# Half of the gate's contraction as seven block products of 160 tokens, and the feed-forward in three parts

## The chip, the cores and the metric

The kernel runs on one core of one Trainium2 chip. Its time is the device time of one execution in microseconds. Two executions of the kernel before took 1676.51 and 1676.54 us, so their median is 1676.53 us. A third execution was recorded by the hardware profiler; it took 1677.32 us, and the span from its first to its last instruction is 1675.2 us.

## The reference

One layer of a decoder (a short gated convolution and a sliding-window attention side by side, merged, then a feed-forward) on 256 prompt tokens and 64 sample tokens, 320 in all. What the change touches is the feed-forward at the end:

```python
h = x + merged @ w_o
hn = rms_norm(h, g_ffn)
h = h + (jax.nn.silu(hn @ w_gate) * (hn @ w_up)) @ w_down
```

The model width is 2048, the feed-forward's inner width 5632. Everything is in 32-bit floats.

## The kernel before, in words

**Products by three passes.** Activations are held feature by feature: a tile has 128 features on the partitions and the 320 tokens (`T`) along the free axis. Each 32-bit operand is split into a high part in the matmul's reduced 32-bit format and a low part that holds the remainder (`split_to`: ScalarE copies the high part, VectorE subtracts to get the low one). A product is then three matmuls: high by high, weight high by activation low, weight low by activation high. Each matmul has a stationary operand of 128x128 weights, which is loaded for that matmul alone, also where two matmuls in succession use the same weights.

**`product`** (L127 to L150) computes two output chunks of 128 features for all tokens. It takes the contraction of 2048 features (`KC` = 16 chunks) in four weight tiles of four chunks each. Per weight tile: SyncE starts a transfer of 512 KB into a `wraw` tile (four buffers), ScalarE writes `whi`, VectorE writes `wlo` (three buffers each), and TensorE runs 24 matmuls of 320 tokens. A `wraw` buffer is free for its next transfer when both halves of its split are done; a `whi` or `wlo` buffer is free when the last matmul that reads it is done. The function `passes` orders the matmuls, with the low-weight pass up to three places (`LAG`) behind the others and four of them at the end of a tile.

**The feed-forward** (L894 to L976) goes through the 44 chunks of the inner width in two parts of 28 and 16 chunks (`FH`). In each part it takes two chunks at a time: a gate product (`fg`, 96 matmuls), the SiLU on VectorE and ScalarE (`gs`, `sg`), an up product (`fu`, 96 matmuls), and the result, split, into the big tile `a_t`. After each part `down` (L844) multiplies `a_t` by the down weights, 512 output features per call, and adds the result to the residual stream `hT`. The last call of the second part is written out by itself (L979 to L1047): its weights are prepared ahead in tiles that have come free (`held`), and 128 of the tokens are accumulated by rows in a PSUM bank that stays reserved (`rowacc`).

**PSUM.** `product` and `down` draw on a pool of four banks (`acc`). A second pool, `aux2`, has three banks.

**The order of the work.** The kernel is written against a framework that records the instructions, sorts them per engine with a scheduler of its own before the program runs, and puts in the semaphore waits. On the chip each engine then works through its list in the order that was fixed; ScalarE and VectorE do not overtake a waiting instruction. The framework treats a PSUM bank as a whole: a matmul that writes to a bank waits for earlier reads of it by other engines, whichever columns they read.

**`wo`** (L810 to L829): the product before the feed-forward. Its eviction adds to `hT` and writes the feed-forward's input, scaled by `g_ffn` and split, to `hh_t` and `hl_t`.

Of the kernel before, what the change touches and what calls it, by code (L numbers as in the profile page):

```python
# [36 lines left out]
E0 = D - 512  # L37
TR = T - P
XB = [1, 1, 2, 2, 2, 2, 2, 4]
TOK = [(0, 128), (128, 128), (256, 64)]  # L40


@with_exitstack
def hybrid_layer(ctx: ExitStack, tc: tile.TileContext, a: dict, o: list):
# [18 lines left out]
    def ps_aux(name):  # L63
        return aux[0].tile([P, 512], F32, tag="aux", name=name)
# [120 lines left out]
    rbsq = cst.tile([P, T], F32, name="rbsq")  # L185
    rbq = cst.tile([P, T], F32, name="rbq")

    def rstd_of(ss, shape, name, pool, out=None):

# [38 lines left out]
    vT = zz.tile([P, 2, T], F32, name="vT")  # L228
    vn = [zz.tile([P, DKV], F32, name=f"vn{t}") for t in range(3)]
    xacc = zz.tile([P, T], F32, name="xacc")  # L230
    rel = zz.tile([NBK, NH], F32, name="rel")
    oh = zz.tile([NBK, WIN], F32, name="oh")
    rel_r = zz.tile([NBK, 2, NH], F32R, name="rel_r")
# [573 lines left out]
    rb2 = hp.tile([P, T], F32, name="rb2")  # L807
    hh_t = xp.tile([P, KC, T], F32R, tag="xh", name="hh_t")
    hl_t = xp.tile([P, KC, T], F32R, tag="xl", name="hl_t")
    for mp in range(8):  # L810
        c0 = mp * CW
        ps = product(
            lambda k0, n: load_cols(w_o, k0, n, c0), KC,
            lambda k: m_h[:, k, :], lambda k: m_l[:, k, :], "wo",
        )
        for c in range(2):
            k = mp * 2 + c
            nc.vector.tensor_add(hT[:, k, :], ps[c][:, :T], hT[:, k, :])
            nc.scalar.activation(hh_t[:, k, :], hT[:, k, :], AF.Copy, scale=g_ffn[:, k:k + 1])
            nc.vector.scalar_tensor_tensor(  # L820
                hl_t[:, k, :], hT[:, k, :], g_ffn[:, k:k + 1], hh_t[:, k, :].bitcast(F32),
                op0=ALU.mult, op1=ALU.subtract,
            )
            if k == 0:
                nc.gpsimd.tensor_tensor(hacc, hT[:, k, :], hT[:, k, :], op=ALU.mult)
            else:
                t = tmp("tc", "sq")[:, :T]
                nc.gpsimd.tensor_tensor(t, hT[:, k, :], hT[:, k, :], op=ALU.mult)
                nc.gpsimd.tensor_tensor(hacc, hacc, t, op=ALU.add)  # L829
    mp_.close()  # L830


# [9 lines left out]
    ylow = op.tile([P, E0], F32, name="ylow")  # L842

    def down(half, c0):  # L844

        nf, f0 = FH[half], half * FH[0]
        ps = [ps_acc(u("dn")) for _ in range(4)]
        low = ps_aux(u("dl")) if c0 < E0 else rowacc
        sets = [[k] for k in range(0, nf, 2)]
        sets[-2:] = [sets[-2] + sets[-1]]  # L850
        for i, k0s in enumerate(sets):
            parts = {}
            for k0 in k0s:
                raw = wp.tile([P, 2, 512], F32, tag="wraw", name=u("wraw"), bufs=4)
                nc.sync.dma_start(raw, w_d[c0 // 512, :, f0 + k0:f0 + k0 + 2, :])
                hi = wp.tile([P, 2, 512], F32R, tag="whi", name=u("whi"), bufs=3)
                lo = wp.tile([P, 2, 512], F32R, tag="wlo", name=u("wlo"), bufs=3)
                split_to(hi, lo, raw)
                for j in range(2):
                    parts[k0 + j] = (hi[:, j, :], lo[:, j, :])  # L860
            end = i == len(sets) - 1
            order = [(k, c) for k in parts for c in range(4)]
            if end or i == 0:
                order.sort(key=lambda kc: kc[1])
            for k, c, m in passes(order, end):
                cs = slice(c * P, (c + 1) * P)
                if m == 0:
                    nc.tensor.matmul(  # L868
                        ps[c], parts[k][0][:, cs], a_t[:, k, 0:512], start=k == 0, stop=False
                    )  # L870
                elif m == 1 and c == 0:
                    nc.tensor.matmul(  # L872
                        low, a_t[:, k, 512:], parts[k][0], start=k == 0, stop=k == nf - 1 and c0 < E0
                    )
                elif m == 2:
                    last["mm"] = nc.tensor.matmul(  # L876
                        ps[c][:, :T], parts[k][1][:, cs], a_t[:, k, 0:T], start=False, stop=k == nf - 1
                    )
            if pending and i % 2 == 1:
                with after(last["lo"], last["mm"]):  # L880
                    pending.pop(0)()
        mark["out"] = []
        for c in range(4):
            k = c0 // P + c
            nc.vector.tensor_add(hT[:, k, :], hT[:, k, :], ps[c][:, :T])
            mark["out"].append(nc.vector.tensor_add(hT[:, k, P:T], hT[:, k, P:T], ps[c][:, T:]))
        if c0 < E0:
            ys = ylow[:, c0:c0 + 512]
            if half == 0:
                nc.scalar.activation(ys, low, AF.Copy)  # L890
            else:
                nc.vector.tensor_add(ys, low, ys)

    for half in range(2):  # L894
        f0 = 0 if half == 0 else FH[0]
        nf = FH[half]

        a_big = fp.tile([P, FH[0], 2 * T], F32R, tag="at", name=u("a_t"))
        a_t = a_big[:, :nf, :]
        for fpair in range(nf // 2):  # L900
            c0 = (f0 + fpair * 2) * P
            psg = product(
                lambda k0, n: load_cols(w_g, k0, n, c0), KC,
                lambda k: hh_t[:, k, :], lambda k: hl_t[:, k, :], "fg",
            )
            if half == 0 and fpair == 0:
                pss = ps_aux("pss2")
                over_partitions(pss[:, :T], two_parts(hacc, ("tc", "td")))
                rstd_of(pss[:, :T], [P, T], "r2", hp, out=rb2)
            gs = []  # L910
            for c in range(2):
                t, t2 = tmp("ta", "gs")[:, :T], tmp("tb", "sg")[:, :T]
                nc.vector.tensor_mul(t, psg[c][:, :T], rb2)
                last["sig"] = nc.scalar.activation(t2, t, AF.Sigmoid)
                nc.vector.tensor_mul(t, t, t2)
                nc.vector.tensor_mul(t, t, rb2)
                gs.append(t)
            psu = product(
                lambda k0, n: load_cols(w_u, k0, n, c0), KC,
                lambda k: hh_t[:, k, :], lambda k: hl_t[:, k, :], "fu",  # L920
            )
            for c in range(2):
                nc.vector.tensor_mul(gs[c], psu[c][:, :T], gs[c])
                f = fpair * 2 + c
                last["hi"] = nc.scalar.activation(a_t[:, f, 0:T], gs[c], AF.Copy)
                for t0, t1, d0 in ((P, T, T), (0, P, 512)):
                    last["lo"] = nc.vector.tensor_sub(
                        a_t[:, f, d0:d0 + t1 - t0], gs[c][:, t0:t1], a_t[:, f, t0:t1].bitcast(F32)
                    )
        if half == 1:  # L930
# [4 lines left out]
            yacc = op.tile([P, TR], F32, name="yacc")  # L935

            def row_squares(i, src):
                jk = op.tile([P, 512], F32, tag="jk", name=u("jk"))
                nc.scalar.activation(jk, src, AF.Square, accum_out=ssf[:, i:i + 1])

            def rows_of(c0):
# [27 lines left out]
            with after(last["sig"]):  # L969
                nc.scalar.activation(warm, ones, AF.Sqrt)  # L970

        for c0 in range(0, D if half == 0 else E0, 512):
            down(half, c0)
            if half == 1:
# [4 lines left out]
    nf = FH[1]  # L979
    es = slice(E0, D)  # L980

    held = []
    free = a_big[:, nf:, :].rearrange("p k t -> p (k t)")
    more = xp.tile([P, 4 * KT * CW], F32R, tag="xl", name="more")
    for j in range(nf // 2):
        raw = wp.tile([P, 2, 512], F32, tag="wraw", name=u("wraw"), bufs=4)
        nc.sync.dma_start(raw, w_d[E0 // 512, :, FH[0] + 2 * j:FH[0] + 2 * j + 2, :])
        if j < 5:
            src, n = (free, 2 * j) if j < 3 else (more, 2 * (j - 3))
            hi, lo = (  # L990
                src[:, i * KT * CW:(i + 1) * KT * CW].rearrange("p (k n) -> p k n", k=2) for i in (n, n + 1)
            )
# [160 lines left out]
```

## Time and profile before

| | value |
|---|---|
| median of two executions | 1676.53 us |
| profiled execution | 1677.32 us |
| its span | 1675.2 us |
| mean granted TensorE clock | 0.999 |
| matmuls | 10967 |
| read from memory | 253.3 MB, 154 GB/s over the span |

How to read the rows that follow: times are microseconds from the start of the span unless marked ns. PE is TensorE's matmuls, PEld its loads of stationary operands, DVE VectorE, ACT ScalarE, SPq the queue of SyncE, which starts the transfers. `L141` is a line of the kernel. A group's row gives the line, the engine, the operation, the tile written and the tiles read, partitions x elements, and the count; then the busy time in us, the mean duration of one in ns, and the idle time of the engine just ahead of them. Matmuls are pipelined, so the duration of one (309 ns for 320 tokens) is longer than the distance to the next.

### The profile page before, as it was taken

What the parts mean: (1) busy time and instruction counts of PE and PEld (TensorE: products, weight loads), DVE (VectorE), ACT (ScalarE), POOL (GpSimd) and SP (SyncE); (2) the same over time, 40 slices, a digit from 0 to 9 for tenths busy, and PEclk for the clock granted to TensorE, in tenths of its full rate; (3) what the DMA queues carried; (4) which work ended last, traced back from release to release, by engine and by line L of the source; (5) the groups of instructions that cost most, each with busy time, mean ns of one, the idle gap of its engine ahead of it and who ended that gap; (6) DMA issues with size and microseconds to landing.
All of it is one profiled execution on the core that took longest, in us unless ns stands there. A gap on an engine that the chain in (4) does not pass through costs nothing.

```text
span 1675.2 us, 26334 instructions
## 1 busy us (share of the span) xinstructions
PE 1664.8 (99%) x10967; PEld 1620.0 (97%) x10967; DVE 893.5 (53%) x1293; ACT 650.9 (39%) x861; POOL 79.5 (5%) x120
## 2 busy tenths in 40 slices
PE   9999999999999999999999999999999999999998
PEld 9999999999999999999999999998888999999887
DVE  7779555444444445556555555553444455555556
ACT  6545343333333333334333333333333333334442
POOL 0101311000000002320000000000000000000000
PEclk9999999999999999999999999999999999999999
DMA  7544545544444444444444444444444444444552
GB/s 256 169 154 140 178 137 183 162 149 149 151 152 151 151 149 149 149 148 150 151 151 151 151 150 148 149 148 151 150 151 151 151 150 151 151 152 151 176 164 88
DMA packets 73390, 258.12 MB, mean 154 GB/s; under 512 B 8440, under 2 KB 10920, under 8 KB 73144
## 3 DMA queue, kind: packets, MB, share of 16 engines
q1 hardware_dynamic: 71160, 250.28, 45.1%
q0 software_dynamic: 1968, 5.90, 1.2%
q8 instruction: 86, 1.41, 0.3%
q14 instruction: 32, 0.26, 0.0%
q10 hardware_dynamic: 144, 0.26, 0.0%
HBM read 253.30 MB, written 5.08 MB: 154 GB/s over the span
## 4 chain that ended last, share of the span: by engine, by line
PE 99%; DMA 0%; ACT 0%; SPq 0%; DVE 0%; issue 0%; DVEq 0%
PE fg L141 18%; PE fu L141 18%; PE dn L868 9%; PE ga L141 7%; PE wo L141 7%; PE gc L141 7%; PE dn L876 6%; PE B L141 3%; PE C L141 3%; PE q L141 3%; PE yc L141 3%; PE H L141 3%; PE ya L141 3%; PE dl L872 2%; PE kv L311 1%; PE dn L1011 1%
## 5 line engine op out<-in xcount | busy, mean ns | idle before, releaser
L95 DVE TENSOR_TENSOR wlo<-wraw,whi 128x1024 fp32r<-128x1024 f32 (+1 forms) x459 | 561.8, 1224 | 636.6 <-ACT whi L94 630.0
L94 ACT ACTIVATE whi<-wraw 128x1024 fp32r<-128x1024 f32 (+1 forms) x459 | 485.5, 1059 | 780.0 <-PE dn L868 157.8
L868 PE MATMUL dn<-a_t,whi 128*128 128x512 f32 x640 | 218.8, 394 | 0.0
L141 PE MATMUL fg<-hh_t,whi 128*128 128x320 f32 x704 | 212.4, 309 | 0.0
L141 PE MATMUL fu<-hh_t,whi 128*128 128x320 f32 x704 | 212.4, 309 | 0.0
L141 PE MATMUL fg<-hl_t,whi 128*128 128x320 f32 x704 | 212.3, 309 | 0.0
L141 PE MATMUL fu<-hl_t,whi 128*128 128x320 f32 x704 | 212.3, 309 | 0.0
L141 PE MATMUL fg<-hh_t,wlo 128*128 128x320 f32 x704 | 164.0, 309 | 0.0
L141 PE MATMUL fu<-hh_t,wlo 128*128 128x320 f32 x704 | 164.0, 309 | 0.0
L876 PE MATMUL dn<-a_t,wlo 128*128 128x320 f32 x640 | 152.0, 309 | 0.0
L868 PEld LDWEIGHTS dn<-a_t,whi 128*128 128x128 f32 x640 | 119.3, 188 | 23.5
L141 PEld LDWEIGHTS fg<-hh_t,whi 128*128 128x128 f32 x704 | 132.2, 188 | 0.0
L141 PEld LDWEIGHTS fu<-hh_t,whi 128*128 128x128 f32 x704 | 132.2, 188 | 0.0
L141 PEld LDWEIGHTS fu<-hl_t,whi 128*128 128x128 f32 x704 | 132.2, 188 | 0.0
L141 PEld LDWEIGHTS fg<-hl_t,whi 128*128 128x128 f32 x704 | 132.2, 188 | 0.0
L876 PEld LDWEIGHTS dn<-a_t,wlo 128*128 128x128 f32 x640 | 112.4, 188 | 10.9
L141 PEld LDWEIGHTS fg<-hh_t,wlo 128*128 128x128 f32 x704 | 118.5, 188 | 0.0
L141 PEld LDWEIGHTS fu<-hh_t,wlo 128*128 128x128 f32 x704 | 118.5, 188 | 0.0
L141 PE MATMUL ga<-xh_t,whi 128*128 128x320 f32 x256 | 77.3, 310 | 0.0
L141 PE MATMUL gc<-xh_t,whi 128*128 128x320 f32 x256 | 77.3, 310 | 0.0
L141 PE MATMUL ga<-xl_t,whi 128*128 128x320 f32 x256 | 77.3, 310 | 0.0
L141 PE MATMUL gc<-xl_t,whi 128*128 128x320 f32 x256 | 77.3, 310 | 0.0
(310 smaller groups left out, 2748.1 us busy)
## 6 DMA issues: line engine op xcount, KB each, us to landing
wraw<-in_w_in_dram SPq DMA_DIRECT2D x128, 512.0 KB, 3.8
wraw<-in_w_gate_dram SPq DMA_DIRECT2D x88, 512.0 KB, 3.7
wraw<-in_w_up_dram SPq DMA_DIRECT2D x88, 512.0 KB, 3.7
wraw<-in_w_down_dram SPq DMA_DIRECT2D x88, 512.0 KB, 3.4
wraw<-in_w_o_dram SPq DMA_DIRECT2D x32, 512.0 KB, 3.7
wraw<-in_w_conv_out_dram SPq DMA_DIRECT2D x16, 512.0 KB, 3.6
wraw<-in_w_attn_out_dram SPq DMA_DIRECT2D x16, 512.0 KB, 3.5
wraw<-in_w_kv_dram SPq DMA_DIRECT2D x7, 512.0 KB, 7.8
```

The lines of the kernel that those rows point to most:

```text
L94: last["hi"] = nc.scalar.activation(hi, src, AF.Copy)
L95: last["lo"] = nc.vector.tensor_sub(lo, src, hi.bitcast(F32))
L141: last["mm"] = nc.tensor.matmul(ps[c][:, :T], w[:, k, c * P:(c + 1) * P], x(kc), start=(kc == 0 and i == 0), stop=(kc == nk - 1 and i == 2),)
L311: last["mm"] = nc.tensor.matmul(ps[c][:, :T], w[:, k, c * P:(c + 1) * P], x(kc), start=(kc == 0 and m == 0), stop=(kc == KC - 1 and m == 2),)
L868: nc.tensor.matmul(ps[c], parts[k][0][:, cs], a_t[:, k, 0:512], start=k == 0, stop=False)
L872: nc.tensor.matmul(low, a_t[:, k, 512:], parts[k][0], start=k == 0, stop=k == nf - 1 and c0 < E0)
L876: last["mm"] = nc.tensor.matmul(ps[c][:, :T], parts[k][1][:, cs], a_t[:, k, 0:T], start=False, stop=k == nf - 1)
L1011: nc.tensor.matmul(ps[c][:, :2 * TR], held[k][0][:, cs], a_t[:, k, P:512], start=k == 0, stop=False)
```

## The change

In 21 of the 22 gate products (all but the first of the first part), half of the contraction is computed by another scheme. Two contraction chunks and two output chunks form a 2 by 2 grid of weight blocks, and the tokens are halved into two blocks of 160 (`T2`). Strassen's scheme, in the form with shared sums, gives the four results of such a grid from seven block products in place of eight. Four of the eight pairs of contraction chunks (`NS`) go this way, in two weight tiles (`by_seven(0)`, `by_seven(1)`); the other two tiles of a gate product are computed as before (`plain`).

For it the kernel prepares, once, sums and differences of the scaled activations of the first eight chunks (`sums_of`, after the first four `wo` products), and, in each of the two weight tiles of each gate product, four sums of weight blocks (`tw`), which are then split like the weights (`thi`, `tlo`, one buffer each). The seven products of three passes each are 42 matmuls of 160 tokens per weight tile. They accumulate in column ranges of three banks (`pa`, `pb`, `pc`, all three of `aux2`); the plain tiles accumulate in columns 0 to 319 of `pa` and `pb`. One result of the seven is read out by ScalarE, and four short VectorE operations combine it with others, ahead of the last plain tile in the text; two VectorE additions follow after it.

The feed-forward is cut into three parts of 16, 14 and 14 chunks in place of 28 and 16. This frees memory for the sums. The activations for the first weights are scaled into a temporary and split from there; some temporaries move to other tiles.

The core of the diff:

```diff
+    sums = hp.tile([P, 2, NS, 4, T2], F32R, tag="sums", name="sums")
+
+    def sums_of(pair, xs):
+        d = hp.tile([P, 4, T2], F32, tag="tw", name=u("sx"), bufs=2)
+        x0, x1 = xs
+        nc.vector.tensor_sub(d[:, 0], x0[:, T2:], x1[:, T2:])
+        nc.vector.tensor_sub(d[:, 2], x0[:, T2:], x0[:, :T2])
+        nc.vector.tensor_sub(d[:, 1], x0[:, :T2], d[:, 0])
+        nc.vector.tensor_sub(d[:, 3], x1[:, :T2], d[:, 1])
+        split_to(sums[:, 0, pair], sums[:, 1, pair], d)
...
-            nc.scalar.activation(hh_t[:, k, :], hT[:, k, :], AF.Copy, scale=g_ffn[:, k:k + 1])
-            nc.vector.scalar_tensor_tensor(
-                hl_t[:, k, :], hT[:, k, :], g_ffn[:, k:k + 1], hh_t[:, k, :].bitcast(F32),
-                op0=ALU.mult, op1=ALU.subtract,
-            )
+            xs = tmp(("ta", "tb")[c], "xs")[:, :T]
+            nc.scalar.activation(xs, hT[:, k, :], AF.Copy, scale=g_ffn[:, k:k + 1])
+            split_to(hh_t[:, k, :], hl_t[:, k, :], xs)
+            scaled.append(xs)
...
+        if mp < NS:
+            sums_of(mp, scaled)
...
-    FH = (28, 16)
+    FH = (16, 14, 14)
...
+    def gate_product(c0):
+        pa, pb, pc = (ps_aux(u(n)) for n in ("ga_", "gb_", "gc_"))
+        sl = lambda p, i: p[:, i * T2:(i + 1) * T2]
+        P3, P5, P2, Q4, P1, P6, P7 = sl(pb, 0), sl(pb, 2), sl(pa, 0), sl(pa, 1), sl(pa, 2), sl(pc, 0), sl(pc, 1)
...
+        def by_seven(tile_i):
+            raw = raw_tile()
+            mark["load"] = nc.sync.dma_start(raw, w_g[c0 // CW, :, tile_i * KT:(tile_i + 1) * KT, :])
+            r4 = raw.rearrange("p (a k) (n m) -> p a (k n) m", k=2, n=2)
+            tw = hp.tile([P, 2, 4, P], F32, tag="tw", name=u("tw"), bufs=2)
+            rh, rl = (x.rearrange("p (a k) (n m) -> p a (k n) m", k=2, n=2) for x in part_tiles())
+            th, tl = (fp.tile([P, 2, 4, P], F32R, tag=t, name=u(t)) for t in ("thi", "tlo"))
+
+            nc.vector.tensor_add(
+                tw[:, :, 0:2], r4[:, :, 0:1].to_broadcast([P, 2, 2, P]), r4[:, :, 1:3]
+            )
+            nc.vector.tensor_add(tw[:, :, 2], tw[:, :, 0], r4[:, :, 2])
+            nc.vector.tensor_add(tw[:, :, 3], tw[:, :, 2], r4[:, :, 3])
+            split_to(rh[:, :, 1:4], rl[:, :, 1:4], r4[:, :, 1:4])
+            split_to(th, tl, tw)
...
+                for out, bank, w, x in (
+                    (P1, "pa", W(rh, rl, 1), h(k, 0)), (P2, "pa", W(rh, rl, 3), h(k + 1, 0)),
+                    (P3, "pb", W(rh, rl, 2), d(3)), (P5, "pb", W(th, tl, 0), d(0)),
+                    (P7, "pc", W(th, tl, 1), d(2)), (P6, "pc", W(th, tl, 2), d(1)),
+                    (Q4, "pa", W(th, tl, 3), h(k + 1, 1)),
+                ):
+                    seq += [(out, bank, w[0], x[0]), (out, bank, w[0], x[1])]
+                    low.append((out, bank, w[1], x[0]))
...
+        by_seven(0)
+        plain(2, False)
+        by_seven(1)
+
+        p1, nw, n = q[:, 0], q[:, 1], q[:, 2]
+        nc.scalar.activation(p1, P1, AF.Copy)
+        nc.vector.tensor_sub(n, p1, P6)
+        nc.vector.tensor_sub(nw, n, P7)
+        nc.vector.tensor_sub(t0[:, 0:T2], P5, n)
+        nc.vector.tensor_sub(t0[:, T2:T], P5, nw)
+        plain(3, True)
+        nc.vector.tensor_add(t1, pa[:, 0:T], q[:, 0:2].rearrange("p a t -> p (a t)"))
+        nc.vector.tensor_add(t0, pb[:, 0:T], t0)
+        return t0, t1
...
-    for half in range(2):
-        f0 = 0 if half == 0 else FH[0]
-        nf = FH[half]
+    for half, nf in enumerate(FH):
+        f0 = F0[half]
...
-            psg = product(
-                lambda k0, n: load_cols(w_g, k0, n, c0), KC,
-                lambda k: hh_t[:, k, :], lambda k: hl_t[:, k, :], "fg",
-            )
             if half == 0 and fpair == 0:
+                psg = product(
+                    lambda k0, n: load_cols(w_g, k0, n, c0), KC,
+                    lambda k: hh_t[:, k, :], lambda k: hl_t[:, k, :], "fg",
+                )
...
+            else:
+                psg = gts = gate_product(c0)
```

More of the change, by code (lines that the diff above doesn't have):

```diff
@@ L39 @@
 XB = [1, 1, 2, 2, 2, 2, 2, 4]
+T2 = T // 2
+NS = 4
 TOK = [(0, 128), (128, 128), (256, 64)]
@@ L230, in hybrid_layer @@
     xacc = zz.tile([P, T], F32, name="xacc")
+    rbsq = zz.tile([P, T], F32, name="rbsq")
+    rbq = zz.tile([P, T], F32, name="rbq")
     rel = zz.tile([NBK, NH], F32, name="rel")
@@ L815, in hybrid_layer @@
         )
+        scaled = []
         for c in range(2):
@@ L839, in hybrid_layer, with plain @@
     op = ctx.enter_context(tc.tile_pool(name="op", bufs=1))
-    FH = (28, 16)
+    FH = (16, 14, 14)
+    F0 = [sum(FH[:i]) for i in range(len(FH))]
+    END = len(FH) - 1
     ylow = op.tile([P, E0], F32, name="ylow")
+    def gate_product(c0):
+        pa, pb, pc = (ps_aux(u(n)) for n in ("ga_", "gb_", "gc_"))
+        sl = lambda p, i: p[:, i * T2:(i + 1) * T2]
+        P3, P5, P2, Q4, P1, P6, P7 = sl(pb, 0), sl(pb, 2), sl(pa, 0), sl(pa, 1), sl(pa, 2), sl(pc, 0), sl(pc, 1)
+        fresh = {"pa": pa, "pb": pb, "pc": pc}
+        t0, t1 = (tmp("ta", "gs")[:, :T] for _ in range(2))
+        q = fp.tile([P, 3, T2], F32, tag="q", name=u("q"))
+        mm = lambda out, w, x, bank, stop: nc.tensor.matmul(
+            out, w, x, start=fresh.pop(bank, None) is not None, stop=stop, skip_group_check=True
+        )
[13 more added lines that the diff above has]
+            split_to(th, tl, tw)
+            seq, low = [], []
+            for a in range(2):
+                pair = tile_i * 2 + a
+                k = 2 * pair
+                h = lambda k, i: tuple(x[:, k, i * T2:(i + 1) * T2] for x in (hh_t, hl_t))
+                d = lambda i: (sums[:, 0, pair, i], sums[:, 1, pair, i])
+                W = lambda x, y, i: (x[:, a, i], y[:, a, i])
+                for out, bank, w, x in (
[6 more added lines that the diff above has]
+                    low.append((out, bank, w[1], x[0]))
+                    if len(low) > LAG:
+                        seq.append(low.pop(0))
+            for out, bank, w, x in seq + low:
+                last["mm"] = mm(out, w, x, bank, False)
+        def plain(tile_i, end):
+            hi, lo = load_cols(w_g, tile_i * KT, KT, c0)
+            order = [(k, c) for k in range(KT) for c in range(2)]
+            if end:
+                order.sort(key=lambda kc: -kc[1])
+            for k, c, i in passes(order, end):
+                kc = tile_i * KT + k
+                w, x = ((hi, hh_t), (hi, hl_t), (lo, hh_t))[i]
+                last["mm"] = mm(
+                    (pb if c == 0 else pa)[:, 0:T], w[:, k, c * P:(c + 1) * P], x[:, kc, :], None,
+                    end and k == KT - 1 and i == 2,
+                )
+        by_seven(0)
[11 more added lines that the diff above has]
+        return t0, t1
@@ L844, in down @@
     def down(half, c0):
-        nf, f0 = FH[half], half * FH[0]
+        nf, f0 = FH[half], F0[half]
         ps = [ps_acc(u("dn")) for _ in range(4)]
@@ L872, in down @@
                     nc.tensor.matmul(
-                        low, a_t[:, k, 512:], parts[k][0], start=k == 0, stop=k == nf - 1 and c0 < E0
+                        low, a_t[:, k, 512:], parts[k][0], start=k == 0 and (c0 < E0 or half == 0),
+                        stop=k == nf - 1 and c0 < E0
                     )
@@ L901, in hybrid_layer @@
             c0 = (f0 + fpair * 2) * P
-            psg = product(
-                lambda k0, n: load_cols(w_g, k0, n, c0), KC,
-                lambda k: hh_t[:, k, :], lambda k: hl_t[:, k, :], "fg",
-            )
             if half == 0 and fpair == 0:
+                psg = product(
+                    lambda k0, n: load_cols(w_g, k0, n, c0), KC,
+                    lambda k: hh_t[:, k, :], lambda k: hl_t[:, k, :], "fg",
+                )
+                psg = [p[:, :T] for p in psg]
                 pss = ps_aux("pss2")
                 over_partitions(pss[:, :T], two_parts(hacc, ("tc", "td")))
-                rstd_of(pss[:, :T], [P, T], "r2", hp, out=rb2)
+                rstd_of(pss[:, :T], [P, T], "r2", spare, out=rb2)
+                gts = [tmp("ta", "gs")[:, :T] for _ in range(2)]
+            else:
+                psg = gts = gate_product(c0)
             gs = []
             for c in range(2):
-                t, t2 = tmp("ta", "gs")[:, :T], tmp("tb", "sg")[:, :T]
-                nc.vector.tensor_mul(t, psg[c][:, :T], rb2)
+                t, t2 = gts[c], tmp("tb", "sg")[:, :T]
+                nc.vector.tensor_mul(t, psg[c], rb2)
                 last["sig"] = nc.scalar.activation(t2, t, AF.Sigmoid)
@@ L929, in hybrid_layer @@
                     )
-        if half == 1:
+        if half == END:
             ya = xp.tile([P, 2, D], F32, tag="xh", name="ya")
@@ L937, in row_squares @@
             def row_squares(i, src):
-                jk = op.tile([P, 512], F32, tag="jk", name=u("jk"))
+                jk = hp.tile([P, 512], F32, tag="tw", name=u("jk"), bufs=2)
                 nc.scalar.activation(jk, src, AF.Square, accum_out=ssf[:, i:i + 1])
@@ L970, in hybrid_layer @@
                 nc.scalar.activation(warm, ones, AF.Sqrt)
-        for c0 in range(0, D if half == 0 else E0, 512):
+        for c0 in range(0, D if half < END else E0, 512):
             down(half, c0)
-            if half == 1:
+            if half == END:
                 pending.append(lambda c0=c0: rows_of(c0))
                 pending.append(lambda c0=c0: rest_of(range(c0 // P, c0 // P + 4)))
-    nf = FH[1]
+    nf = FH[END]
     es = slice(E0, D)
-    held = []
-    free = a_big[:, nf:, :].rearrange("p k t -> p (k t)")
-    more = xp.tile([P, 4 * KT * CW], F32R, tag="xl", name="more")
+    held, places = [], []
+    more = xp.tile([P, 5 * KT * CW], F32R, tag="xl", name="more")
+    free = hp.tile([P, 5 * KT * CW], F32R, tag="sums", name="free")
+    for x in (more, free, a_big[:, nf:, :].rearrange("p k t -> p (k t)")):
+        places += [
+            x[:, i:i + KT * CW].rearrange("p (k n) -> p k n", k=2)
+            for i in range(0, x.shape[-1] - KT * CW + 1, KT * CW)
+        ]
     for j in range(nf // 2):
         raw = wp.tile([P, 2, 512], F32, tag="wraw", name=u("wraw"), bufs=4)
[L987 to L992, printed above, removed]
+        nc.sync.dma_start(raw, w_d[E0 // 512, :, F0[END] + 2 * j:F0[END] + 2 * j + 2, :])
+        if len(places) > 1:
+            hi, lo = places.pop(0), places.pop(0)
         else:
```

2 lines of the change are left out of this document (removed).

## The prediction

> **What bounds the kernel now.** I read the summary and the chain of waits first, then the chain in one stretch of the feed-forward.
>
> ```profile
> span 1675.2 us, 26334 instructions
> ...
> PE 1664.8 (99%) x10967; PEld 1620.0 (97%) x10967; DVE 893.5 (53%) x1293; ACT 650.9 (39%) x861; POOL 79.5 (5%) x120
> ...
> PE 99%; DMA 0%; ACT 0%; SPq 0%; DVE 0%; issue 0%; DVEq 0%
> ```
>
> ```profile
> 947.94 14.08 PE fu L141 x96
> 962.02 14.08 PE fg L141 x96
> ```
>
> ```profile
> 962.02:976.10 14.08, 14.08 (x98) 14.08 (x98) 7.02 (x10) 5.20 (x7) 0.00 (x0) 1.00 0.43 153
> sum 28.16, PE 28.16 PEld 28.16 DVE 14.50 ACT 10.39 POOL 0.00; mean PE 14.08 PEld 14.08 DVE 7.25 ACT 5.20 POOL 0.00
> ```
>
> The first two rows of the summary say that TensorE works without a break, and the chain is TensorE alone. In the feed-forward a product of 96 matmuls takes 14.08 us, 146.7 ns for each matmul of 320 tokens, with no wait in it. One gate and one up product are 28.16 us (the sum row, its columns PE, PEld, DVE, ACT in order), in which VectorE works 14.5 us and ScalarE 10.4. So the time changes by what TensorE's list changes, and by any wait that the change puts into it.
>
> **TensorE's work.** A gate product keeps 48 of its 96 matmuls and does the other 48 as 84 matmuls of 160 tokens. Whether that saves depends on the distance between two short matmuls, each with its own load. The nearest rows:
>
> ```profile
> 1640.74 0.25 PE L1015 MATMUL dn<-a_t 128*128 128x192 f32 x1
> ...
> 1640.83 0.36 PE L1011 MATMUL dn<-a_t 128*128 128x384 f32 x1
> ...
> 1641.03 0.59 PE L1015 MATMUL dn<-a_t 128*128 128x192 f32 x4
> ...
> 1641.45 0.60 PE L945 MATMUL fa<-ident,xv 128*128 128x128 f32 x4
> ```
>
> ```profile
> 116.80 0.82 PE L518 MATMUL pp<-ident,s 128*128 128x128 f32 x6
> ```
>
> ```profile
> L518 PE MATMUL pp<-ident,s x48: 271/272/330, 116.8 to 174.1; 128*128 128x128 f32 x48
> ```
>
> A single matmul of 192 tokens between longer ones takes 90 ns (1640.74 to 1640.83). Four in a row take 0.42 us (1641.03 to 1641.45); with 90 for the first, 110 for each that follows. Six transposes of 128 columns take 0.82 us; less the last one's 0.27, five distances of 110. So in a run the distance does not fall with the width below about 110 ns: it is the load of the next weights that sets it, and PEld is as busy as PE in the sum row. A `by_seven` tile is a run of 42. I take 111 ns, with 105 (the mean of the four) and 113 as bounds. Per gate product: 84 x 111 ns = 9.32 us in place of 48 x 146.7 ns = 7.04, so 2.28 us more, and in 21 products **47.9 us more**. The bounds give 37 and 51.
>
> [...]
>
> **The wait that the change adds.** The built program's order around one gate product, VectorE's list and then ScalarE's (`8345` the last plain tile, `8389` and `8419` the first two tiles of the up product, `8521` to `8527` the first tile of the *next* gate product):
>
> ```
> wlo_8390<-wraw_8387,whi_8389      whi_8389<-wraw_8387
> tw_8523<-wraw_8521   (three)      whi_8419<-wraw_8417
> wlo_8420<-wraw_8417,whi_8419      thi_8526<-tw_8523
> tlo_8527<-tw_8523,thi_8526        q_8195<-ga__1044_8190   (P1)
> q, q, gs, gs         (the four)   whi_8449<-wraw_8447
> ```
>
> TensorE's list has, behind the second `by_seven` tile, three matmuls of the up product, 12 of the last plain tile into `pa` (they wait for ScalarE's read of P1, from the same bank), three more of the up product, 12 into `pb` (they wait for the four on VectorE). So P1's read is queued behind `thi_8526`, that behind `tw_8523`, and that behind the transfer of `wraw_8521`. The up product's tiles hold all four `wraw` buffers, and the first is free when `wlo_8390` is done: VectorE frees a buffer and then waits for what is loaded into it.
>
> ```profile
> 941.49 1.23 DVE L95 TENSOR_TENSOR wlo<-wraw,whi 128x1024 fp32r<-128x1024 f32 x1 [2.29 <-ACT whi L94]
> 942.75 3.80 SPq L99 DMA_DIRECT2D wraw<-in_w_gate_dram  x2
> ```
>
> ```profile
> SPq L99 <- DVE wlo L95: 62.3, 20, 3.2
> ```
>
> ```profile
> DMA to landing us min/median/max: 3.6/3.7/3.9
> ```
>
> ```profile
> L141 PE MATMUL fg<-hh_t,whi 128*128 128x320 f32 x704 | 212.4, 309 | 0.0
> ```
>
> ```profile
> L95 DVE TENSOR_TENSOR wlo<-wraw,whi 128x1024 fp32r<-128x1024 f32 x458 | 561.2, 1225 | 636.4 <-ACT whi L94 629.8 <-PE spp L627 2.3
> L923 DVE TENSOR_TENSOR gs<-fu,gs 128x320 f32<-128x320 f32 x44 | 21.7, 492 | 4.3 <-PE fu L141 3.7
> ...
> L927 DVE TENSOR_TENSOR a_t<-gs,a_t 128x192 fp32r<-128x192 f32 x44 | 15.6, 355 | 11.8 <-ACT a_t L925 11.8
> ...
> L927 DVE TENSOR_TENSOR a_t<-gs,a_t 128x128 fp32r<-128x128 f32 x44 | 12.5, 284 | 0.0
> ...
> L475 DVE TENSOR_TENSOR s<-ps,bias 128x256 f32<-128x256 f32 x16 | 6.2, 424 | 4.2 <-PE ps L466 4.2
> ...
> L1058 DVE TENSOR_TENSOR wraw<-xv,rn 128x768 f32<-128x768 f32 x4 | 3.6, 953 | 0.0
> ...
> L892 DVE TENSOR_TENSOR ylow<-dl,ylow 128x512 f32<-128x512 f32 x3 | 2.1, 692 | 3.8 <-PE dl L872 3.6
> ```
>
> ```profile
> L94 ACT ACTIVATE whi<-wraw 128x1024 fp32r<-128x1024 f32 x458 | 484.9, 1060 | 780.0 <-PE dn L868 157.8 <-PE fg L141 153.4 <-PE fu L141 145.3
> ...
> L953 ACT ACTIVATE sq<-xv 128x192 f32<-128x192 f32 x15 | 5.4, 359 | 14.7 <-DVE xv L1026 5.8 <-DVE yacc L965 4.7 <-DVE xv L886 4.2
> ```
>
> The transfers wait for VectorE's split (row SPq), start 0.03 us after it ends (942.72 to 942.75), and land 3.6 to 3.9 us later. I take 0.04 us for each hand-over, 0.32 us for a VectorE operation of 160 (between the 0.284 at 128 and 0.355 at 192) and 0.34 for ScalarE's (0.359 at 192).
>
> Let E be the end of the second `by_seven` tile's 42 matmuls. They begin at E-4.66. The plain tile ahead of them ends in four matmuls of low weights, so the last that reads its `whi` begins 5 x 0.147 before E-4.66, at E-5.40, and is done at E-5.09 (309 ns). Into that buffer goes the up product's first `whi`: E-5.05 to -3.99. Its `wlo` on VectorE: E-3.95 to -2.72. The transfer starts at E-2.69 and lands at **E+1.01**. The three weight sums (0.69, 0.42, 0.42) end at E+2.66, `thi` at E+3.76, P1's read at E+4.12. TensorE goes on at E+4.16; its three matmuls of the up product lasted to E+0.44. **Wait: 3.72 us.** The 12 into `pa` and the next three end at E+6.36. VectorE meanwhile does `wlo_8420` (to E+3.91), `tlo` (to E+5.16) and the four (to E+6.53); the 12 into `pb` begin at E+6.57, 0.21 us late. Together 3.93 us. It falls on each gate product that is followed by another gate product: 21 less the last of each part, 18. **18 x 3.93 = 70.7 us.** In the three others no such transfer stands in VectorE's list ahead of P1; I take 0.2 us each. A landing of 3.6 or 3.9 gives -2 or +4 us. A shorter distance makes E earlier against the landing, by 42 x 6 ns = 0.25 us at 105, so the wait gives 4.5 us back of the 10.6 saved.
>
> **The other edits.** VectorE's work per `by_seven` tile is 0.69 + 0.42 + 0.42 + 0.95 + 1.23 = 3.7 us in place of 1.23, and the combining costs 4 x 0.32 + 2 x 0.49 = 2.3; a gate and an up product then hold 14.5 + 5.0 + 2.3 = 21.8 us of it in 28.16 + 2.28 + 3.9 = 34.3, so it does not become the bound. ScalarE's, at most 10.4 + 2 x 1.06 + 0.34 = 12.9, does not either. `sums_of` adds 4 x 0.32 + 1.23 us of VectorE to each of four `wo` products of 14 us; were it not covered, 10 us. Three parts mean four more calls of `down`; in the trace no matmul waits between two calls of `down` or at the end of the first part, so nothing. The last call by itself has 14 chunks instead of 16: eight pairs of matmuls of 384 and 192 become pairs of 512 and 320, and four matmuls of 512 by rows fall away; both are under 1 us and opposite. Zero; none of this can gain.
>
> **The sum.** 47.9 + 70.7 + 0.6 = 119 us on the profiled execution's 1677.3: 1796.5; the median of the runs is 0.8 us lower. I say **1796 us**, 7.1% slower. By its bounds 1786 to 1806.
>
> **The rivals.**
>
> *The clock falls in the waits* (slower still).
>
> ```profile
> 1.19 3.70 PE L258 MATMUL wm<-busy 128*128 128x256 bf16 x20 [1.19 <-DVE ones L176]
> 4.93 1.13 PE L311 MATMUL kv<-xh_t,whi 128*128 128x320 f32 x4
> ...
> 10.41 0.42 PE L311 MATMUL kv<-xh_t,whi 128*128 128x320 f32 x1 [1.41 <-ACT whi L94]
> 10.67 0.31 PE L311 MATMUL kv<-xl_t,whi 128*128 128x320 f32 x1
> 10.81 0.31 PE L311 MATMUL kv<-xh_t,whi 128*128 128x320 f32 x1
> ```
>
> At the start 20 matmuls, 13 of 256 columns and 7 of 128, take 3.74 us: 1130 columns per us, where 320 in 146.7 ns are 2180. TensorE starts at half speed for about 3.7 us. If each wait brings that back, 18 x 1.85 = 33 us are added: 1829. Against it: after the 1.41 us wait at 10.41 the distances are back at 0.15 at once, and the granted clock in the row of the window is 1.00. For it: 3.7 us is longer than any wait in the trace. 12%. [...]
>
> *The transfer is hidden* (the landing is earlier, or the order leaves slack that I don't see), so that the load distance alone counts: 1677.3 + 47.9 = 1725. The list speaks against it. 9%.
>
> *The load does not bind in a long run.* A line through 90 ns at 192 and 146.7 at 320 gives 76 at 160; the 1764 matmuls take 134 us, 14 less than the 148 now. But E then comes 42 x 35 ns = 1.5 us earlier against the landing, and the wait is 18 x 5.4 = 97: 1760. 6%.
>
> *The other side, not slower:* the same 76 ns, with the transfer hidden: 1663, 0.8% faster. It decides if the distance is under 84 ns, where 84 matmuls equal the 48. The trace has 90 ns for a single short matmul and 110 in a run, so 3%.
>
> **How the numbers follow.** The forecast holds 64%, the clock 12%, the hidden transfer 9%, the unbound load 6%, the other side 3%; 6% for what I have not seen, mostly slower. The range takes in the forecast, the clock and the unbound load with its wait: 1758 to 1832, 82%. What can be told from no change is 2%, 34 us, so up to 1710 counts as the same: faster 0.01, same 0.04, slower 0.95.
>
> **What would show it.** Right: the groups of 160 tokens about 111 ns apart in the timeline; in each gate product a gap of 3.7 us on TensorE ahead of `ga` of 320 tokens, released by ScalarE's read of P1; VectorE idle 3.8 us ahead of the weight sums, released by a transfer. Wrong: no such gap (hidden transfer), distances under 90 ns, or distances near 290 ns for 320 tokens after the gaps (the clock).

## The result, and the profile after

The changed kernel took 1824.27 us (median of 1823.1 and 1825.44), against 1676.53 before: 1.088 times as long, 95% interval 1.0861 to 1.0896. The profiled execution is the one of 1825.44 us. Its summary, with each engine's busy time, share of the span and count of instructions, then the shares of the chain of waits, two groups of instructions and one kind of transfer (count, size, median us to landing):

```profile
span 1823.5 us, 28327 instructions
...
PE 1755.3 (96%) x11719; PEld 1704.9 (93%) x11719; DVE 1052.4 (58%) x1642; ACT 694.7 (38%) x944; POOL 77.8 (4%) x120
...
PE 90%; DMA 4%; DVE 3%; ACT 2%; issue 1%; SPq 0%; ACTq 0%; DVEq 0%
...
L96 ACT ACTIVATE thi<-tw 128x1024 fp32r<-128x1024 f32 x42 | 44.5, 1059 | 62.6 <-DVE tw L893 57.6
L889 DVE TENSOR_TENSOR tw<-wraw 128x512 f32<-128x512 f32 x42 | 28.9, 688 | 67.0 <-DMA wraw<-in_w_gate_dram 67.0
...
wraw<-in_w_gate_dram SPq DMA_DIRECT2D x88, 512.0 KB, 3.5
```

The chain was TensorE alone before. Now transfers, VectorE and ScalarE hold 9% of it. The two group rows say where: VectorE idles 67.0 us ahead of the 42 first weight sums, all of it for transfers, and ScalarE idles 57.6 us for the sums. The chain through one gate product (start, length, what was being done or waited for; rows of under 0.1 us left out) has the same steps as the prediction's walk:

```profile
916.28 1.07 ACT whi L96
917.37 1.24 DVE wlo L97
918.62 3.64 DMA wraw<-in_w_gate_dram
922.29 0.70 DVE tw L889
923.01 0.43 DVE tw L892
923.47 0.44 DVE tw L893
924.09 0.89 issue
924.98 0.30 ACT q L934
925.32 3.50 PE ga__1164_9165 L877 x12
928.82 0.43 PE fu L143 x3
929.25 1.76 PE gb__1165_9166 L877 x12
```

Read it from the top: the split of the up product's first tile, the transfer that may start only then, the three weight sums, `thi` (the "issue" row), P1's read (`q`), and only then TensorE. One row doesn't fit: 12 matmuls into `ga` take 3.50 us, the same 12 into `gb` 1.76. The timeline around another of these waits (start, length, engine, operation, the count, idle time before it and its releaser) and the granted clock (the column behind POOL) in three windows of 3.4 us around it show why:

```profile
847.27 0.28 PE L877 MATMUL ga__1084_8515<-hh_t,thi 128*128 128x160 f32 x1
...
847.38 0.28 PE L877 MATMUL ga__1084_8515<-hl_t,thi 128*128 128x160 f32 x1
...
847.83 0.28 PE L877 MATMUL ga__1084_8515<-hh_t,tlo 128*128 128x160 f32 x1
...
847.94 0.35 PE L143 MATMUL fu<-hh_t,whi 128*128 128x320 f32 x1
...
848.28 0.31 PE L143 MATMUL fu<-hh_t,whi 128*128 128x320 f32 x1
848.85 0.69 DVE L889 TENSOR_TENSOR tw<-wraw 128x512 f32<-128x512 f32 x1 [3.58 <-DMA wraw<-in_w_gate_dram]
...
850.58 1.06 ACT L96 ACTIVATE thi<-tw 128x1024 fp32r<-128x1024 f32 x1 [3.17 <-DVE tw L893]
851.54 0.28 ACT L934 ACTIVATE q<-ga__1084_8515 128x160 f32<-128x160 f32 x1
...
851.88 0.64 PE L877 MATMUL ga__1084_8515<-hh_t,whi 128*128 128x320 f32 x1 [3.29 <-ACT q L934]
...
852.31 0.47 PE L877 MATMUL ga__1084_8515<-hl_t,whi 128*128 128x320 f32 x1
...
852.58 0.47 PE L877 MATMUL ga__1084_8515<-hh_t,whi 128*128 128x320 f32 x1
```

```profile
843.09:846.50 3.41, 3.41 (x33) 3.41 (x31) 1.23 (x1) 1.07 (x2) 0.00 (x0) 1.00 0.17 40
846.50:849.92 3.42, 2.09 (x18) 1.82 (x16) 1.03 (x2) 0.91 (x1) 0.00 (x0) 1.00 0.39 137
849.92:853.30 3.38, 1.42 (x5) 1.42 (x6) 3.24 (x6) 1.25 (x2) 0.00 (x0) 0.53 0.22 46
```

Ahead of the wait the short matmuls start 0.11 us apart. After the wait of 3.29 us those of 320 tokens start 0.27 us apart, where before the change it was 0.147: half speed. The granted clock was 1.00 in the window in which TensorE fell idle and 0.53 in the next; the half clock itself began at 850.10.

From the start times of all matmuls (a wait counts from 0.147 us after the last start ahead of it, which makes it about 0.15 us longer than the idle time that the rows list) the span's growth, 1823.5 - 1675.2 = 148.3 us, divides so:

| part | count and size | us |
|---|---|---|
| short matmuls | 1764 at 110.76 ns in place of 1008 at 146.7 | +47.5 |
| wait ahead of `ga` | 18 of 3.13 to 3.70 us, mean 3.43 | +61.8 |
| 320-token matmuls at half speed after the wait | 300, each 126 ns longer | +37.8 |
| sum | | 147.1 |

This leaves 1.2 us for everything else. The row on half speed is the prediction's first rival, whose sign it named: distances near 290 ns after the gaps.

### The profile page after: what moved, and what is told of

Read it like the earlier page. It is cut to its first block, busy times and chain, and to the rows that moved or that the text cites. A ratio compares the mean times of both kernels' runs of the same rounds, so it can differ in the third digit from the quotient of the medians.

```text
span 1823.5 us, 28327 instructions
## 1 busy us (share of the span) xinstructions
PE 1755.3 (96%) x11719; PEld 1704.9 (93%) x11719; DVE 1052.4 (58%) x1642; ACT 694.7 (38%) x944; POOL 77.8 (4%) x120
## 4 chain that ended last, share of the span: by engine, by line
PE 90%; DMA 4%; DVE 3%; ACT 2%; issue 1%; SPq 0%; ACTq 0%; DVEq 0%
PE fu L143 17%; PE dn L968 8%; PE ga L143 6%; PE wo L143 6%; PE gc L143 6%; PE dn L977 5%; DMA wraw<-in_w_gate_dram 3%; PE B L143 3%; PE C L143 3%; PE q L143 3%; PE yc L143 3%; PE H L143 3%; PE ya L143 3%; PE dl L972 2%; PE kv L313 1%; DVE wlo L97 1%
## 5 line engine op out<-in xcount | busy, mean ns | idle before, releaser
L97 DVE TENSOR_TENSOR wlo<-wraw,whi 128x1024 fp32r<-128x1024 f32 (+2 forms) x459 | 549.7, 1198 | 497.7 <-ACT whi L96 485.6
L96 ACT ACTIVATE whi<-wraw 128x1024 fp32r<-128x1024 f32 (+2 forms) x459 | 475.6, 1039 | 849.7 <-PE dn L968 157.9
L143 PE MATMUL fu<-hl_t,whi 128*128 128x320 f32 x704 | 216.8, 314 | 0.0
L143 PEld LDWEIGHTS fu<-hl_t,whi 128*128 128x128 f32 x704 | 136.2, 193 | 0.0
L143 PE MATMUL wo<-m_h,whi 128*128 128x320 f32 x256 | 77.2, 309 | 0.0
L143 PE MATMUL wo<-m_l,whi 128*128 128x320 f32 x256 | 77.2, 309 | 0.0
L96 ACT ACTIVATE thi<-tw 128x1024 fp32r<-128x1024 f32 x42 | 44.5, 1059 | 62.6 <-DVE tw L893 57.6
L889 DVE TENSOR_TENSOR tw<-wraw 128x512 f32<-128x512 f32 x42 | 28.9, 688 | 67.0 <-DMA wraw<-in_w_gate_dram 67.0
L143 PE MATMUL gc<-xh_t,wlo 128*128 128x320 f32 x256 | 59.7, 310 | 0.0
L143 PE MATMUL ga<-xh_t,wlo 128*128 128x320 f32 x256 | 59.7, 310 | 0.0
```

Of the source, the lines that this page charges most:

```text
L96: last["hi"] = nc.scalar.activation(hi, src, AF.Copy)
L97: last["lo"] = nc.vector.tensor_sub(lo, src, hi.bitcast(F32))
L143: last["mm"] = nc.tensor.matmul(ps[c][:, :T], w[:, k, c * P:(c + 1) * P], x(kc), start=(kc == 0 and i == 0), stop=(kc == nk - 1 and i == 2),)
L889: nc.vector.tensor_add(tw[:, :, 0:2], r4[:, :, 0:1].to_broadcast([P, 2, 2, P]), r4[:, :, 1:3])
```

## The experiments

What had to be told apart: whether the wait comes from the order of P1's read behind a transfer; whether the slow matmuls come from idle time on TensorE; whether the load sets the 111 ns; and whether anything else in the change costs time. The kernel before, run beside them, took 1676.69 us (median of 13 runs) for the experiments "read first", "filled" and "parts alone", and 1676.64 for the other four. All but "parts alone" were run once.

**P1's read first.** The read of P1 and the four operations of one gate product are put ahead of the next one's weight sums and their split; nothing is added or left out.

```diff
+    combined = []
...
-            nc.vector.tensor_add(
-                tw[:, :, 0:2], r4[:, :, 0:1].to_broadcast([P, 2, 2, P]), r4[:, :, 1:3]
-            )
+            with after(*combined):
+                nc.vector.tensor_add(
+                    tw[:, :, 0:2], r4[:, :, 0:1].to_broadcast([P, 2, 2, P]), r4[:, :, 1:3]
+                )
...
-            split_to(th, tl, tw)
+            with after(*combined):
+                split_to(th, tl, tw)
...
-        nc.scalar.activation(p1, P1, AF.Copy)
+        m1 = nc.scalar.activation(p1, P1, AF.Copy)
...
-        nc.vector.tensor_sub(t0[:, T2:T], P5, nw)
+        m2 = nc.vector.tensor_sub(t0[:, T2:T], P5, nw)
+        combined[:] = [m1, m2]
```

> The changed kernel, but each gate product reads P1 and does its four short operations ahead of the next gate product's weight sums and their split. Theory (load distance 47 us, 18 waits of 3.4 us, half clock after each wait 38 us): TensorE waits no more than 0.2 us ahead of the last plain tile, the granted clock is 1.00, the short matmuls stay 111 ns apart, 1726 us (1722 to 1732). Rival A, the half clock comes from the runs of short matmuls and not from the waits: no waits, clock still near 0.975, about 1764 us. Rival B, something else than the order of the lists holds the last plain tile: waits over 1 us remain, 1750 us or more.

Measured: 1729.1 us, clock 0.999. Its chain at the place where the change had its wait:

```profile
930.25 0.48 PE fu L143 x3
930.73 1.94 PE ga__1204_9490 L879 x12
932.66 1.76 PE gb__1205_9491 L879 x12
```

No wait, and full speed on both sides. So the order alone makes the wait, and with the wait the half clock goes too: 95 us of the 148 hang on where one short ScalarE read, and the four VectorE operations that need it, stand in their lists. What stays is 47.5 us for the short matmuls and 3.9 us in 42 leftover gaps of 0.09 us.

**The wait filled.** The order stays as in the change; after the second `by_seven` tile TensorE gets 28 matmuls on constant data, whose result nobody reads.

```diff
+        wf = ps_acc(u("wf"))
+        for _ in range(28):
+            nc.tensor.matmul(wf[:, :CW], busy[:, :P], busy, start=True, stop=True)
```

> The changed kernel with 28 matmuls of 256 columns on a constant tile behind the second tile of seven products in each of the 21 gate products; they go to a PSUM tile that nobody reads. They lie in the wait in 18 gate products and are extra work (3.1 us each) in three. Theory, the idle time brings the clock down: the wait for P1's read is as long as it was, but filled for 3.1 us; clock 1.00; 1824 - 38 + 9 = 1795 us. Rival A, the runs of short matmuls bring it down: clock still near 0.975, 1833 us.

Measured: 1813.38 us, clock 0.999. Its timeline on TensorE:

```profile
846.16 0.27 PE L877 MATMUL ga__1086_8573<-hh_t,tlo 128*128 128x160 f32 x1
846.27 3.23 PE L935 MATMUL wf<-busy 128*128 128x256 bf16 x28
850.20 0.41 PE L877 MATMUL ga__1086_8573<-hh_t,whi 128*128 128x320 f32 x1 [0.70 <-ACT q L938]
850.46 0.31 PE L877 MATMUL ga__1086_8573<-hl_t,whi 128*128 128x320 f32 x1
850.60 0.31 PE L877 MATMUL ga__1086_8573<-hh_t,whi 128*128 128x320 f32 x1
```

P1's read is as late as in the change (from the last short matmul, at 846.16, to `ga` 4.04 us; in the change, from 847.83, 4.05), but from the second matmul on the distance is 0.15 us again (850.46 to 850.60). Adding 588 matmuls made the kernel 11 us faster. So the idle time brings the clock down, not the switch of width or the late read. The expected time was 18 us too low. With the filler in the list the scheduler no longer put the 3 + 3 matmuls of the up product in and behind the wait. The first three now come on top of the wait (3 x 0.147 x 18 = 7.9 us). In place of the other three stands a wait of 0.25 us ahead of `gb` (18 x 0.25 = 4.5 us). Together that is 12.4 us; some 6 us of the miss stay open.

**Half the filler.** 14 matmuls in place of 28, to leave a shorter idle time.

```diff
-        for _ in range(28):
+        for _ in range(14):
```

> e3_fill with 14 matmuls in place of 28, so that about 2.4 us of each wait stay idle. Theory, the clock falls when TensorE's work in a window of about 3.4 us is low, idle or not in full: it falls behind some of the 18 waits, mean clock 0.98 to 0.995, time 1813 - 5 + 10 to 30 = 1818 to 1838 us. Rival, only a window that is idle in full brings it down: no half clock, 1.00, 1808 us.

Measured: 1817.55 us, clock 0.992. The group rows of the first matmuls into `ga` of two gate products of it (count, then busy us and mean ns of one, then idle us before them and its releaser):

```profile
L877 PE MATMUL ga__1004_7865<-hh_t,whi 128*128 128x320 f32 x8 | 3.0, 382 | 2.2 <-ACT q L938 2.2
...
L877 PE MATMUL ga__1127_8885<-hh_t,whi 128*128 128x320 f32 x8 | 2.5, 323 | 2.3 <-ACT q L938 2.3
```

An idle time of 2.2 us was followed by slow matmuls in the first, one of 2.3 us by full speed in the second. Of the 18 waits 7 were followed by a window of half clock (7 x 3.41 = 24 us). The idle time alone does not decide, and 2.2 us can be enough. The time is 0.5 us below the range that the theory gave; the clock is inside it.

**A buffer of its own.** The other way to take the transfer from behind the up product: the `by_seven` tiles load into a buffer that no up tile uses. To make room, `tw` has one buffer in place of two. With the buffer in the pool of the other weight tiles and two buffers for `tw` the kernel does not fit: an earlier stage needs 33 KB per partition where 29.4 KB are left.

```diff
-            raw = raw_tile()
+            raw = fp.tile([P, KT, CW], F32, tag="w7", name=u("w7"), bufs=1)
...
-            tw = hp.tile([P, 2, 4, P], F32, tag="tw", name=u("tw"), bufs=2)
+            tw = hp.tile([P, 2, 4, P], F32, tag="tw", name=u("tw"), bufs=1)
```

> The changed kernel, but the weight tiles that go by seven products are loaded into a buffer of their own (and the sums' temporary has one buffer in place of two, to make room), so their transfer no longer waits for the up product's first split. The weight sums move ahead of that split in VectorE's list; the split of the sums stays ahead of P1's read on ScalarE. Theory: what remains of the wait is that split, about 1.1 us for each of 18 gate products, too short to bring the clock down: 1677 + 47 + 20 = 1744 us, clock 1.00. Rival, the transfer was not what held the read: waits of 3 us or more and 1815 us or more.

Measured: 1740.51 us, clock 0.999. The chain at the wait:

```profile
870.62 0.42 ACT thi L96
871.04 0.55 issue
871.59 0.29 ACT q L934
871.92 2.03 PE ga__1124_8840 L877 x12
```

P1's read still stands behind `thi`, but `thi` no longer waits for a transfer: the wait shrinks to 0.63 us (expected 1.1), in 20 gate products in place of 18, and the clock stays up. Over all places the waits are 14.9 us; with 47.5 for the short matmuls that is 62.4 of the span's 1738.6 - 1675.2 = 63.4.

**Half the columns.** The corrected order of the first experiment, and 63 of a gate product's 84 short matmuls with 64 of the 128 weight columns. Half of the sums of these 63 are left out.

```diff
-            for out, bank, w, x in seq + low:
-                last["mm"] = mm(out, w, x, bank, False)
+            for i, (out, bank, w, x) in enumerate(seq + low):
+                m = P if tile_i == 0 and i < 21 else 64
+                last["mm"] = mm(out[:m], w[:, :m], x, bank, False)
```

> e1_read_first, but 63 of the 84 short matmuls of each gate product use only the first 64 columns of their stationary operand and write 64 partitions (so half of their sums is left out). Theory, the load of 128 columns sets the distance of 111 ns: with half the columns the distance falls to what the 160 tokens take, 76 to 82 ns, and the time to 1729 - 1323 x 31 ns = 1688 us (1680 to 1695). Rival, each short matmul has a fixed distance whatever is loaded: 111 ns and 1729 us.

Measured: 1683.4 us. The timeline inside a `by_seven` tile:

```profile
823.03 0.24 PE L879 MATMUL ga__1084_8515<-hh_t,whi 128*64 128x160 f32 x1
823.10 0.24 PE L879 MATMUL ga__1084_8515<-hl_t,whi 128*64 128x160 f32 x1
823.18 0.24 PE L879 MATMUL gc__1086_8517<-sums,tlo 128*64 128x160 f32 x1
823.25 0.31 PE L879 MATMUL gb__1085_8516<-sums,whi 128*64 128x160 f32 x2
```

The same 160 tokens, 0.07 us apart in place of 0.11; over all 1323 of them the mean is 74 ns. What changed is the columns of the stationary operand and, with them, the partitions written. The writing does not need the 111 ns: in the next experiment, too, a short matmul that writes all 128 partitions is followed by the next after 0.07 us (826.19 and 826.26) where a long one stands ahead of it. So the load sets the distance of 111 ns.

**Short matmuls spread among long ones.** If the load binds, a short matmul beside a long one might have its load hidden by the long one. The short ones of a `by_seven` tile are spread evenly among the 24 matmuls of a plain tile, and P1 is read at the end.

```diff
-        by_seven(0)
-        plain(2, False)
-        by_seven(1)
+        def spread(short, long):
+            n, done = len(short), 0
+            for i, s in enumerate(short):
+                last["mm"] = mm(*s)
+                while done < len(long) and done * n < (i + 1) * len(long) - n // 2:
+                    last["mm"] = mm(*long[done])
+                    done += 1
+            for s in long[done:]:
+                last["mm"] = mm(*s)
+
+        spread(by_seven(0), plain(2, False))
+        spread(by_seven(1), plain(3, True))
```

> The changed kernel, but the matmuls of each seven-product tile are spread among those of a plain tile, about one of 320 tokens for two of 160, and P1 is read at the end of the gate product. It has waits of its own, since the second tile's sums have one buffer (about 1 us in each of 21 gate products). What is asked is the distances. Theory, every matmul needs its load of 110 ns and a longer neighbour's time is not lent to it (in the kernel before, 384 and 192 in turn take 285 ns, which is 175 + 110): 42 short and 24 long together take 8.2 us as they do in a row, and the time is near 1750 us. Rival, a short one between long ones takes 90 ns and the long one stays at 147: 0.5 us less for each pair of tiles, and the time near 1728 us.

Measured: 1727.59 us, clock 0.999, with no waits. The timeline of TensorE:

```profile
826.00 0.35 PE L877 MATMUL ga__1084_8515<-hh_t,whi 128*128 128x320 f32 x1
826.19 0.24 PE L877 MATMUL gb__1085_8516<-sums,whi 128*128 128x160 f32 x1
826.26 0.28 PE L877 MATMUL gb__1085_8516<-sums,thi 128*128 128x160 f32 x1
826.37 0.34 PE L877 MATMUL ga__1084_8515<-hl_t,whi 128*128 128x320 f32 x1
826.56 0.24 PE L877 MATMUL gb__1085_8516<-sums,thi 128*128 128x160 f32 x1
826.63 0.35 PE L877 MATMUL gb__1085_8516<-hh_t,whi 128*128 128x320 f32 x1
```

The distances look as if something were won: from a short one to the next 0.07. But the step from a long one to a short one is now 0.19. A long and two short ones take 0.37 us (826.00 to 826.37), which is 0.147 + 2 x 0.111; a long and one short 0.26 (826.37 to 826.63), which is 0.147 + 0.111. So the price of a short matmul is the same, and the time agrees with the rival's number only because the waits of about 1 us that the theory put on top did not occur. Against the first experiment it is 1.5 us faster, less than that one's 3.9 us of leftover gaps.

**Parts alone.** The changed kernel with every gate product computed as before and without the sums of activations: the three parts, the scaling through a temporary and the moved temporaries are left.

```diff
-                psg = gts = gate_product(c0)
+                psg = product(
+                    lambda k0, n: load_cols(w_g, k0, n, c0), KC,
+                    lambda k: hh_t[:, k, :], lambda k: hl_t[:, k, :], "fg",
+                )
...
-        if mp < NS:
-            sums_of(mp, scaled)
```

> The changed kernel with every gate product as before (no seven products, no sums): what is left is the feed-forward in three parts of 16, 14 and 14 chunks and the scaled activations through a temporary. Theory: the same as before within 2 us, 1675 to 1679 us. Rival: three parts cost or gain something of their own, over 5 us.

Measured in three rounds: 1676.38 us (10 runs) against 1676.69, ratio 1.0001, 95% interval 0.9992 to 1.0011. The edits that are left cost nothing that can be measured.

No version that computes all of the seven products' sums beats the kernel before; the best two, 1727.6 and 1729.1 us, are 3.0% and 3.1% slower.

Not tried: a wait of the same length with only matmuls of 320 tokens ahead of it, so the share that the short matmuls have in bringing the clock down is open; and one load shared by the two high-weight matmuls that follow each other with the same weights, which aims at the 111 ns itself.

## Why the prediction was right, and what it put at the wrong chance

The measured time is inside the range and on the forecast side, but 28 us above the number: the likeliest case was not quite the one that happened.

*The load binds: right.* Forecast +47.9 us, measured +47.5, at 110.8 ns for the assumed 111. With 64 of the 128 columns loaded the distance came to 74 ns, so the cause is shown.

*The wait ahead of the last plain tile into `pa`: right in place, cause and count, 8% too long.* Forecast 3.72 us, measured 3.43 on average. The transfer landed in 3.5 us (median) in place of the assumed 3.7, and ScalarE took up P1's read about 0.1 us ahead of the listed end of `thi`. Over 18 waits it is 61.8 us against 67.0. (The prediction's walk is 0.02 us short at P1's read, 3.76 + 0.04 + 0.34 being 4.14; that changes nothing.)

*The wait ahead of `pb`: did not occur.* Forecast 0.21 us each. The four operations on VectorE were sized too long: with hand-overs they were given 1.37 us, and around the wait at 851.88 they took 1.13 (852.81 to 853.94), each starting before the one ahead of it had ended. They were done 2.06 us after the first matmul into `pa`, where 15 matmuls at full speed take 2.2. So this wait would not have come at full clock either. At half speed TensorE left them more time still (3.50 us for the 12 in the chain above, in place of 1.76). The term is worth 3.8 us.

*The clock: the failed step.* The forecast kept the clock at 1.00 and gave its fall 12%, at 18 x 1.85 = 33 us. It fell behind all 18 waits and cost 37.8 us. The price was nearly right and the chance wrong. The argument against it was that TensorE was back at full speed after a wait of 1.41 us; that the waits forecast were longer than any in the trace was noted beside it and given too little weight. The windows show what was missed. In the window 846.50 to 849.92 TensorE was still at work for 2.09 of 3.42 us, 1.44 us of that (to 847.94) on short matmuls, whose 160 tokens, as an estimate from the distance with half the columns, fill 74 of the 111 ns; half clock followed in the next window. Laid so that it ends where the half clock began (846.69 to 850.10), the window has 1.90 us of work in 3.41. Here the wait did not have to fill a window.

In the record of the granted clock, half clock lasted 3.41 us nine times and 6.83 us nine times, and its starts lie whole steps of 3.41 us apart, wherever the wait lay (781.83 and 850.10 are 20 steps apart). It followed 18 of 18 waits, after idle times of 2.97 to 3.54 us.

*The other edits at zero: right*, to within 0.2% (parts alone). The sums of activations, which that run leaves out, were not measured by themselves; they fall within the 1.2 us that the table leaves over.

*The rivals.* The hidden transfer (1725) was the time of the kernel with P1's read first, 1729.1: the mechanism holds, but the order of the change rules it out, as the prediction said. The unbound load (76 ns) and the other side, not slower, fall with the measured 110.8 ns: at 84 ns 84 short matmuls would equal the 48 they replace, and with 128 columns to load no arrangement brought a short matmul clearly below 111, counted over whole groups.

## What to carry to other kernels

Before work is saved by cutting matmuls into narrower ones, compare the distance of a narrow pair of load and matmul in a run, taken from the trace, with what is replaced: here 84 x 111 ns against 48 x 147 ns, where counting tokens would give 84 x 160 against 48 x 320. When a step is added that frees a PSUM bank, follow the reading engine's list backwards from that step to the first thing that waits for a transfer; a read of 0.3 us behind one cost 95 us here. Price a repeated TensorE wait with the half speed behind it as well as with its length: here half clock followed 18 of 18 waits of 2.97 to 3.54 us and 7 of 18 of 2.0 to 2.5 us.

## What the runs showed of the hardware

The clock fell also after windows that were only partly idle (1.90 of 3.41 us at work ahead of 850.10). The starts of half clock, whole steps of 3.41 us apart, divide the changed kernel's time into windows. As an estimate of the time in which matmuls stream, count 74 ns for one of 160 tokens (the distance with half the columns) and 147 for one of 320 (the distance before the change). In the feed-forward of the changed kernel the 18 windows at full clock that were followed by half clock then hold 0.00 to 0.37 of streaming, and no other window at full clock less than 0.54. This is a border in one trace, not a general threshold: a window near 229 us, mostly of matmuls of 32 columns, holds 0.33 by a count of this kind and was not followed by half clock. By length: idle times up to 1.0 us (the filled wait, the buffer of its own; mean clock 0.999 in both) were never followed by it, those of 2.0 to 2.5 us (half the filler; 0.992) in 7 cases of 18, those of the changed kernel, 2.97 to 3.54 us (0.974), in 18 of 18.

A wait for one buffer can stop TensorE by way of engines that have time to spare: VectorE was at 58% and ScalarE at 38% in the changed kernel, and the chain ran through both of them, because each took its list in order.

The distance to the next matmul depends on the one before: in the spread version, on average, 186 ns from 320 to 160 tokens, 74 from that one to a second of 160, and from this one 111 back to 320. Read singly, these rows would price a short matmul at 74 ns; only the sum over a whole group shows 111.
